# A gated-linear-attention block on one core: two column blocks of its input projection cut into groups of 512 columns, some of their steps by block sums

## The chip, the cores and the metric

The kernel runs on one core of one Trainium2 chip. The metric is the device time of one execution in microseconds, as the median of several runs. The span in a profile is the time from the first to the last instruction of the core; the execution that was profiled took a little longer than its span.

## The reference

One layer (DEPTH is 1) of a pre-RMSNorm residual trunk, on 256 tokens of width 2048, in float32:

```
def reference(x, ...):
    h = x
    h = h + _gla_mixer(_rmsnorm(h, gla_norm), gla_w_in, gla_w_gate_up, gla_b_gate, gla_o_norm, gla_w_out)
    h = h + _sq_relu_mlp(_rmsnorm(h, mlp_norm), mlp_w_up, mlp_w_down)
    return _rmsnorm(h, final_norm)

def _gla_mixer(h, ...):
    q, k, v, r, g_low = split(h @ w_in)                # 1024, 1024, 2048, 2048, 16 columns
    log_a = log_sigmoid(g_low @ w_gate_up + b_gate) / 16
    # chunks of 64 tokens, 4 heads of 256 (keys) and 512 (values)
    state = d_c * state + k_dec^T v ;  o = q state     # scan over 4 chunks
    o = o * rsqrt(mean(o * o) + EPS) * o_norm
    return (o * silu(r)) @ w_out                       # 2048 x 2048

def _sq_relu_mlp(h, w_up, w_down):
    a = relu(h @ w_up)                                 # 8192 columns
    return (a * a) @ w_down
```

## The kernel before

All 256 tokens are kept on the chip, as two tiles of 128 tokens (`t` = 0, 1). The 2048 rows of a weight are 16 tiles of 128 (`kt`), or 8 pairs of them (`kp`). Every float32 weight is loaded to a tile `raw`, split by ScalarE into a rounded part `hi` (L121) and by VectorE into the rest `lo = raw - hi` (L134, L168), and multiplied on TensorE in three terms: x.hi with w.hi, x.hi with w.lo, x.lo with w.hi. There are six `raw` tiles, and five `hi` and five `lo` slots; a step that wants a tile waits until an earlier step has let go of it. Weights are loaded through SyncE's queue, in order.

The stages, in order of time: the first value half and the gate's low-rank columns (`in_w_vg`, to about 50 us); two key halves and two query halves of 512 columns (`turned`, to about 140 us); the second value half with the scores (to about 190 us); the first gate half with attention (to about 252 us); the second gate half, in which the transposing of the attention output begins (to about 287 us); four output groups of 512 columns (`out_group`, to about 374 us); then the MLP, which the change doesn't touch.

The second value half and both gate halves are calls of `natural`: 1024 columns, one 128-row tile of weights a step, four PSUM banks (two token tiles x two halves of 512 columns). A product on TensorE has 128 rows, 128 tokens and 256 columns, so a step has 2 x 4 x 3 = 24 of them.

`out_group` takes a pair of row tiles and 512 columns a step. A plain step has 24 products as well. A step "by sums" multiplies the 2 x 2 blocks (row tiles by token tiles, row tiles by halves of 256 columns) with seven products in place of eight (Winograd's form of Strassen's method), each in three terms: 21 products. It needs sums of the activations (eight forms, of which four are the blocks themselves), and sums of the weights. One sum of the weights is made by a load that adds to `raw`, issued by GpSimd (L798, after the plain load has landed); the others are made by VectorE (`weight_sums`, L231 and L232), in place, after three quarters of the raw tile have been split for the products that need no sum. Then the sums are split in a second pair of slots (L121 with 512 columns, L829) and the remaining four block products, the "second part" of the step, follow after the products of the next step. Products of the sums collect in two banks of their own, which are combined on ScalarE and VectorE when the last of them is done (L835 to L840) and added to the two banks of the group (L843).

For six of the output groups' steps, the first and the sixth or so of groups 1 to 3, the weight sums are prepared earlier (`make_sums`, `MADE_OUT`, `MADE_AT`): a piece of `w_out` is loaded, summed and split in an earlier stage (L248 to L258), written to DRAM, and read back later (`pre`, L793), ready for TensorE.

Work beside the products is put between the steps: `pump` runs one entry of `side` and one of `jobs` after each step (of a row tile in `turned` and `natural`), in the order that these lists have. `issue_after` fixes the order of instructions on an engine; otherwise the order on each engine is made when the program is built. Attention (`attend`) has 6 products for the first token tile and 12 for the second of each of four heads, and then a chain ScalarE (square sum, L619), VectorE (L620), GpSimd (a power, L401), VectorE (L623) for its normalization. `xe` holds copies of two row tiles of x at another address; some steps after scores, transposes or a change of stage use them (`EVEN`, `row_x`).

The residual `h` is loaded at the start (L391), into 16 KB a partition that it keeps to the end; its square sum gives the first normalization (`token_ssq`, L404). It is first needed when the first output group's banks begin with it (`begin_out`, L726).

Of the kernel before, what the change touches and what calls it, by code (L numbers as in the profile page):

```python
# [32 lines left out]
P = 128  # L33
T = 256
NT = T // P
D = 2048
# [32 lines left out]
def tile_gla_mlp(ctx, tc, x, xt, cols, w_vg, w_in, w_gate, w_out, w_up, w_down, final_norm, out):  # L69
# [4 lines left out]
    mid = ctx.enter_context(tc.tile_pool(name="mid", bufs=1))  # L74
    wpool = ctx.enter_context(tc.tile_pool(name="wpool", bufs=5))
# [98 lines left out]
    def halves(o, x, w, first, last):  # L174

        n = w.shape[-1]
        for c in range(0, n, T) if n % T == 0 else (0,):
            m = slice(c, c + T) if n % T == 0 else slice(0, n)
            nc.tensor.matmul(o[:, m], x, w[:, m], start=first and c == 0, stop=last, skip_group_check=True)  # L179
# [82 lines left out]
    def make_all():  # L262
        pair = lambda w, c0, g: w[c0 : c0 + 2 * P, g * GT : (g + 1) * GT].rearrange("(i p) c -> p i c", p=P)
        todo = [make_sums((None, g, kp), pair(w_out, 2 * kp * P, g)) for g, kp in MADE_OUT]
        todo += [make_sums((ROUNDS - 1, g, kp), pair(w_down, (ROUNDS - 1) * MR + 2 * kp * P, g)) for g, kp in MADE_DOWN]
        jobs.extend([lambda: None] * 3 * (KT - 1))
        for at, (high, low) in zip(MADE_AT, todo):
            jobs[at], jobs[at + 1] = high, low
# [78 lines left out]
    x_loads = {0: 1, 1: 3, 3: 6, 6: 9, 9: 12, 12: KT}  # L347

    def input_tile(kt):
# [14 lines left out]
        return (pieces, pieces) if kt == 0 else ([(0, 512), (512, WMAX)], pieces) if kt == 1 else None  # L364
# [11 lines left out]
    h = const.tile([P, NT, D], F32, name="h")  # L376
# [11 lines left out]
    def load_h(t, half):  # L388
        c = slice(half * G, (half + 1) * G)
        with tc.issue_after(last_load[0].ins):  # L390
            nc.sync.dma_start(out=h[:, t, c], in_=x[t * P : (t + 1) * P, c])  # L391
# [6 lines left out]
    ms1 = st.tile([P, NT], F32, name="ms1")  # L398
# [4 lines left out]
    def token_ssq(t):  # L403
        nc.scalar.activation(  # L404
            kab[:, 0].rearrange("p b c -> p (b c)"), h[:, t, :], AF.Square,
            accum_out=ms1[:, t : t + 1],
        )
# [12 lines left out]
    side.extend([clear_gate] + [nothing] * 8 + [load_gate, lambda: load_h(0, 0), lambda: load_h(0, 1)])  # L420
    side.extend([lambda: (load_h(1, 0), load_h(1, 1), split_gate())])
# [126 lines left out]

    for half in range(2):
        acc = turned(stream_x, w_in, half * GT, even=())  # L550
# [9 lines left out]
    def scores(hd, banks=None):  # L560
# [3 lines left out]
        def mm(o, k, q):  # L564
            for c in range(2):
                nc.tensor.matmul(o, kab[:, k[0], c0 + c, k[1] : k[1] + P], q(qt[:, c0 + c]), start=c == 0, stop=c == 1)  # L566
# [21 lines left out]

    def two_scores(hd):
        spare = [psum_bank(i, "aux") for i in list(acc_free)[:2]]  # L590
# [3 lines left out]
    side.extend([nothing] * 4 + [lambda: two_scores(0), nothing, lambda: two_scores(2)])  # L594
# [30 lines left out]
    side.extend([lambda: None] + [lambda hd=hd, t=t: attend(hd, t) for hd in range(HEADS) for t in range(NT)])  # L625
# [14 lines left out]
    S3, S2, S1, S4, A12, A11, A22, A21 = range(8)  # L640

    def form_sums(f, tt):
        tt(f[:, S3], f[:, A21], f[:, A11], ALU.subtract)
        tt(f[:, S2 : S1 + 1], f[:, A22 : A22 + 1].to_broadcast([P, 2, P]), f[:, 0::7], ALU.add)
        tt(f[:, S4], f[:, A12], f[:, S2], ALU.subtract)

    FORMED = (0, 1, 6, 7)
    in_forms = lambda a: a.rearrange("p (f s) -> p f s", f=8)
# [35 lines left out]
    acc = natural(once_x, rows(w_in, 4 * KEYW), G, HALF, order=even_at(0, 6))  # L684
    flush()
    gate_out(acc, 0)
# [32 lines left out]
    two = lambda a: a.rearrange("p (f s) -> p f s", f=2)  # L719
# [15 lines left out]
    side.extend([nothing] * 7 + [lambda: begin_out(0)])  # L735
# [10 lines left out]
    @contextmanager  # L746
    def then_mm():
        with ExitStack() as order:
            if last_mm[0]:
                order.enter_context(tc.issue_after(last_mm[0]))  # L750
            yield
        last_mm[0] = newest[0]

    made_o = []

    def out_group(g, order, summed, between):

        tt = nc.vector.tensor_tensor
        banks = [out_banks[g, t] for t in range(NT)]
        sums_banks = []  # L760
        begun = set()
        pending = None
        block = lambda i, n=1: slice(i * T, (i + n) * T)

        def product(bank, o, a, w, n, last=False):
            for x in a[: 2 - n]:
                for d in range(0, w.shape[-1], T):
                    newest[0] = nc.tensor.matmul(  # L768
                        bank[:, o + d : o + d + T], x, w[:, d : d + T],
                        start=bank in sums_banks and bank.name not in begun, stop=last, skip_group_check=True,  # L770
                    ).ins
                    begun.add(bank.name)

        def products(these, w, last=False):
            with then_mm():
                for n in range(2):
                    for bank, o, a, c in these:
                        product(bank, o, a, w[n][:, c], n, last and n == 1)

        for step, kp in enumerate(order):  # L780
            by = kp in summed
            ready = made.get((None, g, kp))
            raw = raw_tile()[:, : 2 * GT]
            src = w_out[2 * kp * P : 2 * (kp + 1) * P, g * GT : (g + 1) * GT].rearrange("(i p) c -> p i c", p=P)
            if ready is not None:
                if not made_o:
                    made_o.extend(big.tile([P, 4 * G + 64], F32R, tag="C", name="pre")[:, : 4 * G].rearrange("p (b i c) -> b p i c", b=2, i=2))
                ready_in = made_o[0]
                made_o.reverse()
                last_load[0] = nc.sync.dma_start(out=raw[:, T:GT], in_=src[:, 0, T:])  # L790
                last_load[0] = nc.sync.dma_start(out=raw[:, GT:], in_=src[:, 1])
                for i in range(2):
                    last_load[0] = nc.sync.dma_start(out=ready_in[:, i].bitcast(F32), in_=ready[i])  # L793
                ready = [ready_in[:, i] for i in range(2)]
            elif by:
                for i in range(2):
                    last_load[0] = nc.sync.dma_start(out=raw[:, i * GT : (i + 1) * GT], in_=src[:, i])
                nc.gpsimd.dma_start(out=raw[:, :T], in_=src[:, 0, T:], accum_op=ALU.add)  # L798
            else:
                last_load[0] = nc.sync.dma_start(out=raw.rearrange("p (i c) -> p i c", i=2), in_=src)  # L800
            w = parts(raw, 2 * GT, slots(), [(T * by, 2 * GT)])
            if by:
# [572 lines left out]
```

## Time and profile before

| | |
|---|---|
| median of 3 runs | 1042.85 us (1042.48 to 1043.14) |
| the profiled execution | 1043.0 us |
| its span | 1041.1 us |
| granted TensorE clock | 0.999 |
| instructions in the span | 23253 |
| DMA traffic | 241.48 MB, mean 232 GB/s |

The page of the profile gives, for each engine, its busy time and share of the span. PE is TensorE's matmuls, PEld its weight loads, DVE is VectorE, ACT ScalarE, POOL GpSimd, SP SyncE; a "q" behind the name is the queue that issues DMAs. A row of a group of instructions reads: line, engine, operation, written tile <- read tiles, shapes, count | busy us, mean ns of one | idle us of the engine just before them, and what ended that idle time. A row of a timeline begins with start and length in us. A row of a stage view reads: stage, its length, then busy time (and count of instructions) of PE, PEld, DVE, ACT and POOL, the granted clock, the share of the 16 DMA engines and GB/s. A row of DMA issues ends with KB of each and the median us to landing.

### The profile page before, as it was taken

To read this page: it belongs to the slowest core of one execution; us is meant where nothing else is said; L and a number is where in the kernel's file an instruction comes from. 1 tells how busy PE (TensorE), PEld (TensorE's weight loads), DVE (VectorE), ACT (ScalarE), POOL (GpSimd) and SP (SyncE) were. 2 spreads that over 40 slices of the span, in tenths; PEclk is the share of its full clock that TensorE was granted. 3 is DMA by queue.
4 is the path that set the end of the run, shared out by engine and by line. 5 is a ranking of instruction groups with operands and counts; after the bars stand their busy time and mean duration, and the time that the engine had idled before them with its cause. 6 is when DMAs were issued, how large, how long until landed. Compare 5 with 4: busy or idle time off the path is not lost.

```text
span 1041.1 us, 23253 instructions
## 1 busy us (share of the span) xinstructions
PE 1032.0 (99%) x9046; PEld 1031.4 (99%) x9046; DVE 874.6 (84%) x1191; ACT 738.5 (71%) x1091; POOL 126.9 (12%) x173
## 2 busy tenths in 40 slices
PE   9999999999999999999999999999999999999997
PEld 9999999999999999999999999999999999999997
DVE  6668665667698876989999999999999999999887
ACT  7675554546586755677779788778788778778685
POOL 0000000120100001111111111111111111111000
PEclk9999999999999999999999999999999999999999
DMA  9966676665979976678887888887888888887772
GB/s 339 331 193 190 196 253 213 219 222 167 317 233 296 301 250 197 180 211 232 225 247 226 230 234 224 240 236 224 248 225 228 239 229 228 240 232 220 231 245 84
DMA packets 123742, 241.48 MB, mean 232 GB/s; under 512 B 11200, under 2 KB 28480, under 8 KB 123504
## 3 DMA queue, kind: packets, MB, share of 16 engines
q1 hardware_dynamic: 103616, 216.11, 64.7%
q0 software_dynamic: 19296, 22.29, 11.6%
q10 hardware_dynamic: 720, 1.60, 0.4%
q8 instruction: 71, 1.16, 0.4%
q14 instruction: 39, 0.32, 0.1%
HBM read 231.56 MB, written 8.39 MB: 230 GB/s over the span
## 4 chain that ended last, share of the span: by engine, by line
PE 98%; DMA 1%; issue 0%; ACT 0%; SPq 0%; DVE 0%; POOLq 0%; POOL 0%; DVEq 0%
PE up L923 33%; PE acc L923 28%; PE acc L179 18%; PE acc L768 8%; PE acc L222 6%; PE aux L222 2%; PE aux L179 1%; PE aux L667 1%; PE aux L566 1%; DMA raw<-in_w_vg 1%; ACT sqf L1262 0%; SPq L171 0%; PE acc L467 0%; SPq L356 0%; DVE hf L1334 0%
## 5 line engine op out<-in xcount | busy, mean ns | idle before, releaser
L121 ACT CAST hi<-raw 128x768 fp32r<-128x768 f32 (+4 forms) x630 | 507.0, 834 | 207.1 <-DVE raw L231 61.5
L134 DVE TENSOR_TENSOR lo<-raw,hi 128x768 fp32r<-128x768 f32 (+3 forms) x226 | 236.0, 1051 | 82.9 <-ACT hi L121 71.8
L923 PE MATMUL acc<-hi,act 128*128 128x256 f32 x1696 | 247.7, 276 | 0.0
L923 PE MATMUL up<-hh,hi 128*128 128x256 f32 x1024 | 238.7, 276 | 0.0
L923 PE MATMUL up<-hl,hi 128*128 128x256 f32 x1024 | 238.7, 276 | 0.0
L168 DVE TENSOR_TENSOR lo<-raw,hi 128x1024 fp32r<-128x1024 f32 x160 | 194.7, 1219 | 29.1 <-ACT hi L121 28.6
L923 PEld LDWEIGHTS acc<-hi,act 128*128 128x128 f32 x1696 | 217.6, 188 | 0.0
L923 PEld LDWEIGHTS up<-hl,hi 128*128 128x128 f32 x1024 | 192.2, 188 | 0.0
L923 PEld LDWEIGHTS up<-hh,hi 128*128 128x128 f32 x1024 | 192.2, 188 | 0.0
L1133 POOL DMA_DIRECT2D raw<-in_w_down x112 | 97.1, 867 | 518.0 <-DMA raw<-in_w_down 225.3
L1193 DVE TENSOR_TENSOR lo<-raw,hi 128x1024 fp32r<-128x1024 f32 x112 | 136.4, 1218 | 1.1 <-ACT hi L121 1.1
L923 PE MATMUL up<-hh,lo 128*128 128x256 f32 x1024 | 137.0, 276 | 0.0
L923 PE MATMUL acc<-lo,act 128*128 128x256 f32 x848 | 133.8, 276 | 0.0
L923 PEld LDWEIGHTS up<-hh,lo 128*128 128x128 f32 x1024 | 125.7, 188 | 0.0
L923 PEld LDWEIGHTS acc<-lo,act 128*128 128x128 f32 x848 | 113.4, 188 | 0.0
L179 PE MATMUL acc<-hi,xA 128*128 128x256 f32 (+1 forms) x736 | 105.5, 278 | 0.6 <-ACT hi L121 0.6
L179 PEld LDWEIGHTS acc<-hi,xA 128*128 128x128 f32 x736 | 94.2, 188 | 1.0 <-ACT hi L121 1.0
L232 DVE TENSOR_TENSOR raw<-raw 128x512 f32<-128x512 f32 x128 | 88.3, 690 | 3.4
L231 DVE TENSOR_TENSOR raw<-raw 128x256 f32<-128x256 f32 x128 | 54.1, 423 | 11.5 <-DMA raw<-in_w_out 8.5
L179 PE MATMUL acc<-lo,xA 128*128 128x256 f32 (+1 forms) x368 | 61.8, 278 | 0.0
L179 PEld LDWEIGHTS acc<-lo,xA 128*128 128x128 f32 x368 | 51.0, 188 | 0.0
L222 PE MATMUL acc<-xA,hi 128*128 128x256 f32 x288 | 49.2, 276 | 0.0
(194 smaller groups left out, 1241.4 us busy)
## 6 DMA issues: line engine op xcount, KB each, us to landing
raw<-in_w_up SPq DMA_DIRECT2D x128, 512.0 KB, 4.5
raw<-in_w_down SPq DMA_DIRECT2D x224, 256.0 KB, 4.4
raw<-in_w_in SPq DMA_DIRECT2D x80, 512.0 KB, 4.5
raw<-in_w_down POOLq DMA_DIRECT2D x112, 128.0 KB, 5.1
raw<-in_w_out SPq DMA_DIRECT2D x22, 512.0 KB, 5.1
raw<-in_w_down SPq DMA_DIRECT2D x16, 512.0 KB, 5.0
raw<-in_w_vg SPq DMA_DIRECT2D x14, 520.0 KB, 8.6
raw<-in_w_out SPq DMA_DIRECT2D x26, 256.0 KB, 5.4
```

The source lines that it names most:

```text
L121: last_hi[0] = nc.scalar.copy(to, raw)
L134: last_lo[0] = nc.vector.tensor_tensor(lo[:, s], raw[:, s], hi[:, s].bitcast(F32), op=ALU.subtract)
L168: last_lo[0] = nc.vector.tensor_tensor(to[1], dst, to[0].bitcast(F32), op=ALU.subtract)
L179: nc.tensor.matmul(o[:, m], x, w[:, m], start=first and c == 0, stop=last, skip_group_check=True)
L222: nc.tensor.matmul(o, u[:, i, s], m, start=kt == 0 and n == 0 and j % 2 == 0, stop=kt == KT - 1 and n == 2, skip_group_check=True,)
L231: nc.vector.tensor_tensor(u[:, 2], u[:, 0], u[:, 2], op=ALU.subtract)
L232: return nc.vector.tensor_tensor(u[:, 1::2], u[:, 1::2], u[:, 2:3].to_broadcast([P, 2, T]), op=ALU.subtract)
L566: nc.tensor.matmul(o, kab[:, k[0], c0 + c, k[1] : k[1] + P], q(qt[:, c0 + c]), start=c == 0, stop=c == 1)
L768: newest[0] = nc.tensor.matmul(bank[:, o + d : o + d + T], x, w[:, d : d + T], start=bank in sums_banks and bank.name not in begun, stop=l ...
L923: newest[0] = nc.tensor.matmul(o, x, w, start=first, stop=last, skip_group_check=True).ins
L1133: nc.gpsimd.dma_start(out=raw[:, :T], in_=src[:, 0, T:], accum_op=ALU.add)
L1193: last_lo[0] = nc.vector.tensor_tensor(to[1][:, :G], u, to[0][:, :G].bitcast(F32), op=ALU.subtract)
```

## The change

The second value half and the first gate half (2 x 1024 columns) become four groups of 512 columns, V0, V1, G0 and G1, each of eight steps over a pair of row tiles, by the same function that serves the output groups (now `group`). For three pairs of x (0, 1 and 4) the eight forms are made from the transposed x during the first stage (`make_x`); the four sums among them are kept in the place of the residual, the blocks are x itself. Two steps of V0 and three of V1, G0 and G1 are by sums; each of these steps loads its first 128 x 256 piece a second time, adding, through GpSimd. The scores stand between the steps of V0, six of the eight attention blocks between those of G0, the last two in G1. The results of the sums are combined in a buffer where the last quarter of the residual will lie.

The residual is loaded in the second gate half, after its steps 6 to 9, in four pieces into the four places that the three x forms and the combining buffer had. The square sum at the start reads a copy of x loaded at the old time into the keys' buffer.

Five steps of the output groups are prepared in place of six (the first step of output group 1 is not), three of them in the second query half and two in the second gate half as before. At the start one tile of x in place of two is loaded ahead of the second weights, and the third weights are split in three pieces.

```
-    MADE_OUT = ((1, 1), (1, 6), (2, 1), (2, 6), (3, 1), (3, 6))
-    MADE_AT = (1, 5, 19, 24, 36, 40)
+    MADE_OUT = ((1, 6), (2, 1), (2, 6), (3, 1), (3, 6))
+    MADE_AT = ((0, 5, 10), (6, 10))
...
-    x_loads = {0: 1, 1: 3, 3: 6, 6: 9, 9: 12, 12: KT}
+    x_loads = {0: 1, 1: 2, 2: 4, 4: 7, 7: 10, 10: 13, 13: KT}
...
-        return (pieces, pieces) if kt == 0 else ([(0, 512), (512, WMAX)], pieces) if kt == 1 else None
+        loads = {0: pieces, 1: [(0, 512), (512, WMAX)], 2: [(0, WMAX)]}
+        return (loads[kt], pieces) if kt in loads else None
...
-    h = const.tile([P, NT, D], F32, name="h")
+    x_forms = {kp: shared.tile([P, G], F32R, tag=f"h{i}", name="xf")... for i, kp in enumerate(X_FORMED)}
...
+    def load_x(t, half):
+        c = slice(half * G, (half + 1) * G)
+        with tc.issue_after(last_load[0].ins):
+            nc.sync.dma_start(out=k_rows[:, t, c], in_=x[t * P : (t + 1) * P, c])
+
+    def load_h(t, half):
+        h[t, half] = shared.tile([P, G], F32, tag=f"h{2 * half + t}", name="h")
+        with tc.issue_after(last_load[0].ins):
+            nc.sync.dma_start(out=h.get((t, half)), in_=x[t * P : (t + 1) * P, half * G : (half + 1) * G])
...
+    def make_x(kp):
+        f = in_forms(wpool.tile([P, G], F32, tag="more", name="form", bufs=1))
+        for i in range(2):
+            kt = 2 * kp + i
+            nc.scalar.activation(f[:, A12 + 1 - i :: 2], xr[:, kt, :]..., AF.Copy, scale=g1(kt))
+        form_sums(f, lambda o, x, y, op: nc.vector.tensor_tensor(o, x, y, op=op))
+        sh, sl = (x_forms[kp][:, i] for i in range(2))
+        nc.scalar.copy(sh, f[:, :A12])
+        nc.vector.tensor_tensor(sl, f[:, :A12], sh.bitcast(F32), op=ALU.subtract)
...
-    make_all()
-    acc = natural(row_x, rows(w_in, 3 * KEYW), G, HALF, order=even_at(9, 11))
-    flush()
-    for t in range(NT):
-        for c in range(2):
-            put_v(acc[t][c], 512, t, G + 512 * c)
+    def x_group(n, c0, order, summed, between, put, rows_of={}):
+        def combine(p16, p57):
+            nc.scalar.copy(comb_x[:, 1::2], two(p16))
+            nc.scalar.copy(comb_x[:, 0::2], two(p57))
+            # four sums of 256 columns on VectorE
+        def put_all(banks):
+            for t in range(NT):
+                o = comb_x[:, 2 * t : 2 * t + 2]
+                nc.vector.tensor_tensor(o, two(banks[t]), o, op=ALU.add)
+                put(o.rearrange("p f s -> p (f s)"), t)
...
+    V0 = (5, 0, 6, 2, 4, 3, 7, 1), (0, 4)
+    V1 = (2, 5, 0, 3, 4, 6, 1, 7), (0, 4, 1)
+    G0 = (2, 5, 0, 3, 4, 6, 1, 7), (0, 4, 1)
+    G1 = (2, 0, 5, 4, 3, 1, 6, 7), (0, 4, 1)
+    x_group(0, 3 * KEYW, *V0, {
+        **{i: lambda i=i: [f() for f in rest[2 * i : 2 * i + 2]] for i in range(2)},
+        2: lambda: two_scores(0), 4: lambda: two_scores(2),
+    }, at_of_v(0), FIRST)
+    x_group(1, 3 * KEYW + GT, *V1, {}, at_of_v(GT))
...
+    x_group(2, 4 * KEYW, *G0, {i + 1: f for i, f in enumerate(attends[:6])}, gate_x(0), {2: FIRST[2]})
+    x_group(3, 4 * KEYW + GT, *G1, {i: f for i, f in enumerate(attends[6:])}, gate_x(GT))
...
-    acc = natural(once_x, rows(w_in, 4 * KEYW), G, HALF, order=even_at(0, 6))
-    flush()
-    gate_out(acc, 0)
...
-    side.extend([nothing] * 7 + [lambda: begin_out(0)])
+    side.extend([nothing] * 3 + [lambda i=i: load_h(i % 2, i // 2) for i in range(4)] + [lambda: begin_out(0)])
```

The body of `group` is that of `out_group` before, with what differs between the output and the x groups passed in (the banks, the forms, how the sums are combined and where the result goes).

More of the change, by code (lines that the diff above doesn't have):

```diff
@@ L35 @@
 NT = T // P
+X_FORMED = (0, 1, 4)
 D = 2048
@@ L547, in extend_q @@
         )
+    make = make_all()
     for half in range(2):
+        if half:
+            jobs.extend(next(make))
         acc = turned(stream_x, w_in, half * GT, even=())
```

284 lines of the change are left out of this document (169 added, 115 removed).

## The prediction

> **What bounds the kernel now.** I read the page first (busy shares, then the chain that ended last), then TensorE's own waits, then stages. From the page:
>
> ```profile
> PE 1032.0 (99%) x9046; PEld 1031.4 (99%) x9046; DVE 874.6 (84%) x1191; ACT 738.5 (71%) x1091; POOL 126.9 (12%) x173
> ...
> PE 98%; DMA 1%; issue 0%; ACT 0%; SPq 0%; DVE 0%; POOLq 0%; POOL 0%; DVEq 0%
> ```
>
> TensorE's waits in the whole execution:
>
> ```profile
> core 0 of [0], span 1041.1 us
> engine line waited for: us in total, times, longest us
> PE aux L295 <- DVE ones L292: 1.1, 1, 1.1
> PE acc L179 <- ACT hi L121: 0.6, 2, 0.4
> ```
>
> TensorE is busy 99% of the span, 98% of the chain is its own, and after the warm-up it waits twice, 0.6 us together. So a matmul taken out of the stream shortens the kernel by its full spacing, provided that no new wait appears. A piece of the chain in which nothing interrupts gives the spacing:
>
> ```profile
> 75.20 65.36 PE acc L222 x576
> ```
>
> 65.36 / 576 = 0.1135 us for a 128x128x256 product. The change can save only products, and it can lose only by making TensorE wait or by making its products slower.
>
> **The change part by part.** *Products.* A plain step over a pair of 128-row tiles takes 2 row tiles x 2 token tiles x 2 column quarters x 3 terms = 24 products; a step by sums takes 7 block products x 3 terms = 21. The lists in the code hold 2 + 3 + 3 + 3 = 11 steps by sums (the change's few words say ten). 11 x 3 = 33 products go; 33 x 0.1135 = 3.75 us. Attention, scores and transposes keep their number. With ten steps it would be 3.40 us.
>
> *What VectorE and ScalarE do for a step by sums.* The output groups (287 to 374 us) work this way already, so their rows price it:
>
> ```profile
> L134 DVE TENSOR_TENSOR lo<-raw,hi 128x1024 fp32r<-128x1024 f32 x14 | 16.8, 1219 | 1.2 <-ACT hi L121 0.6 <-DMA pre<-made 0.5
> L134 DVE TENSOR_TENSOR lo<-raw,hi 128x768 fp32r<-128x768 f32 x15 | 14.2, 951 | 0.1
> L829 DVE TENSOR_TENSOR lo<-raw,hi 128x1024 fp32r<-128x1024 f32 x10 | 12.2, 1217 | 1.2 <-ACT hi L121 1.1
> L232 DVE TENSOR_TENSOR raw<-raw 128x512 f32<-128x512 f32 x9 | 6.2, 688 | 0.2
> ...
> L843 DVE TENSOR_TENSOR h<-acc,some 128x512 f32<-128x512 f32 x8 | 5.2, 682 | 0.0
> ...
> L231 DVE TENSOR_TENSOR raw<-raw 128x256 f32<-128x256 f32 x9 | 3.8, 422 | 7.2 <-DMA raw<-in_w_out 7.1
> ```
>
> On VectorE a plain step costs 1.22 us, a step by sums 0.95 + 0.42 + 0.69 + 1.22 = 3.28 us. A group with three of them costs 3 x 3.28 + 5 x 1.22 = 15.9 us, then four combining sums of 256 columns, as L231's (4 x 0.42 = 1.7), two additions to the banks (2 x 0.68 = 1.4) and two evacuations. For these and for attention, from 140 to 260 us:
>
> ```profile
> L623 DVE TENSOR_SCALAR on<-aux,r1k,ors 128x512 f32<-128x512 f32 x8 | 6.5, 808 | 3.5 <-POOL ors L401 3.5
> ...
> L431 DVE SCALAR_TENSOR_TENSOR vl<-acc,r,vh 128x512 fp32r<-128x512 f32 x4 | 2.7, 745 | 0.0
> ```
>
> Two evacuations of values cost 1.5 us (the gate's, two of the 0.68 kind, 1.4), so a group comes to 20.5 us of VectorE against (3 x 21 + 5 x 24) x 0.1135 = 20.8 us of TensorE. In G0 six attention blocks add 6 x 0.81 = 4.9 us to VectorE and 54 products, 6.1 us, to TensorE. On paper VectorE therefore fits with 1 to 7% to spare. In the first value group, with two steps by sums and all the scores, there is more room. Whether such a fit holds in practice is shown by the stretch 287 to 309, the first output group, in the next view:
>
> ```profile
> core 0: us, PE busy (x) PEld busy (x) DVE busy (x) ACT busy (x) POOL busy (x), PEclk, DMA share, GB/s
> 108.00:140.00 32.00, 32.00 (x285) 32.00 (x284) 20.46 (x37) 14.18 (x19) 3.08 (x17) 1.00 0.67 207
> 190.00:252.00 62.00, 62.00 (x549) 62.00 (x548) 41.89 (x57) 33.41 (x49) 9.23 (x12) 1.00 0.67 217
> 248.00:268.00 20.00, 20.00 (x179) 20.00 (x178) 15.95 (x25) 13.54 (x20) 1.64 (x3) 1.00 0.64 218
> 268.00:287.00 19.00, 19.00 (x170) 19.00 (x170) 12.01 (x12) 9.19 (x11) 3.79 (x5) 1.00 0.94 316
> 287.00:309.00 22.00, 22.00 (x196) 22.00 (x195) 21.51 (x34) 17.65 (x30) 1.11 (x2) 1.00 0.71 233
> ```
>
> There VectorE is busy 21.51 of 22.00 us and TensorE still 22.00: four steps by sums and two transposing turns were hidden. The new groups ask for less. I cost the x groups' VectorE and ScalarE work at nothing on the path; it is hidden by the products. If the cover is gone the price is the overhang: TensorE would stand 1 us per group for every 5% that VectorE loses to waits.
>
> *The group for which one prepared step is dropped.* Output group 1 must now form the sums of its first step: 0.42 + 0.69 + 1.22 = 2.33 us more on VectorE, right behind the stretch that is full. How much room is there? VectorE first, then TensorE's first use of the same `lo` tiles (the third row of VectorE opens with the tile for 324.58; the first of the second fence is the one for 305.93):
>
> ```profile
> 304.57 1.22 DVE L134 TENSOR_TENSOR lo<-raw,hi 128x1024 fp32r<-128x1024 f32 x1
> ...
> 319.94 1.21 DVE L829 TENSOR_TENSOR lo<-raw,hi 128x1024 fp32r<-128x1024 f32 x1
> 321.07 5.22 DVE L134 TENSOR_TENSOR lo<-raw,hi 128x1024 fp32r<-128x1024 f32 x5
> ```
>
> ```profile
> 305.93 0.41 PE L768 MATMUL acc<-lo,oth 128*128 128x256 f32 x2
> ...
> 324.58 0.39 PE L768 MATMUL acc<-lo,oth 128*128 128x256 f32 x2
> ```
>
> The tile used at 305.93 is ready at 305.79: 0.14 us of room, the tightest place of this part. The tile used at 324.58 begins at 321.07 and takes 1.22 us, ready at 322.29: 2.29 us of room. Of the 2.33 us added, back-to-back starts are some 7% shorter than durations (from 319.94 to 321.07 is 1.13 for 1.21), so about 2.15 us arrive, and the room shrinks to about 0.1. Bounds: 0 if it fits, 2.3 if the added work comes in a bunch with other late work. I take 0.2.
>
> *The residual loaded late.* Four loads of 128 x 1024 x 4 B, 2.1 MB, now stand in SyncE's queue in steps 6 to 9 of the second gate half, ahead of the output groups' first weights; the early loads at the start stay (into the keys' buffer). From 248 to 287 the rows carry 20 x 0.218 + 19 x 0.316 = 10.4 MB; with 2.1 more, 12.5 MB in 39 us or 320 GB/s, and most of it should come before 268, where the DMA share is 0.64. What the engines can carry is seen at the start:
>
> ```profile
> 0.00:20.00 20.00, 18.36 (x136) 17.93 (x137) 12.66 (x22) 14.21 (x25) 1.77 (x9) 1.00 0.91 337
> 20.00:40.00 20.00, 20.00 (x169) 20.00 (x168) 13.11 (x16) 13.51 (x20) 0.00 (x0) 1.00 1.03 391
> ```
>
> 391 GB/s, so on average it fits. If all of it fell into 268 to 287, 6.0 + 2.1 = 8.1 MB would need 20.7 us at 391 GB/s instead of 19: 1.7 us late, and the group behind it has 0.14 us of room. Bounds 0 and 1.7; I take 0.3. The last of the four also waits until the combining buffer in the same place is free; behind it in SyncE's queue stand weight loads for some 20 us ahead, which is its cover.
>
> *Prepared steps in the second query half.* Three of the five now run there, five 12-product passes apart (5 x 12 x 0.1135 = 6.8 us). Each costs VectorE 0.42 + 0.42 + 0.69 + 1.22 = 2.75 us; the plain steps in 6.8 us cost 2.5 x 1.22 = 3.1. From 108 to 140 VectorE is idle 11.5 of 32 us, so 8.3 us fit. Their traffic, 3 x (0.5 read + 1.05 written) = 4.7 MB, lifts 6.6 MB in that stretch to 11.3, or 354 GB/s. The rate of 391 above holds it. The Trainium skill (DMA: Bandwidth & Descriptors, Specifications) gives about 358 GB/s as a core's share of HBM; by that figure this stretch would just fit too, but 268 to 287 would be late by 3.6 us instead of 1.7. The measured 391 GB/s is over the figure, and I go by it. On the path I take 0 for this part, with 0 and 1 as bounds.
>
> *The start.* One tile of x instead of two is loaded ahead of the second weights:
>
> ```profile
> 6.31 0.91 ACT L370 ACTIVATE xA<-zz,colt 128x256 fp32r<-128x256 f32 x2 [0.80 <-DMA zz<-in_xt]
> 7.38 0.71 ACT L121 CAST hi<-raw 128x256 fp32r<-128x256 f32 x2 [0.16 <-DMA raw<-in_w_vg]
> ```
>
> Both rows wait for DMA, and behind them TensorE has its 0.6 us of waits. 131 KB less at 337 GB/s come 0.39 us earlier. Gain between 0 and 0.6; I take 0.4. Making the sums of x (three times some 2 us on VectorE by the rows for 256 and 512 columns, between 20 and 40 us where it is busy 13.11 of 20) is off the path. The prefetch after that runs ahead of TensorE, so nothing is lost again.
>
> **The sum**, against the profiled execution's 1043.0 us (span 1041.1): -3.75 - 0.4 + 0.2 + 0.3 and 0.2 for small waits at the four group borders = -3.45, so 1039.6. The median of the runs shown is 0.15 lower than the profiled time: 1039.4.
>
> **The rivals.** *A: VectorE becomes the bound in the new groups.* For it: 20.5 against 20.8 us leaves nothing for waits, and from 190 to 252 VectorE idles 20 of 62 us although there is room ahead of it. Against: 287 to 309. If 5% are lost in V1, G0 and G1, 3 us come back: 1042.4, within 0.2% of before.
>
> *B: the handover to the output groups.* The loads fall late (1.7 us) and group 1 has no room (2.3 us): 1039.4 - 0.5 + 4.0 = 1042.9, also no change that can be told. By the page's 358 GB/s it would be 1.9 us more, 1044.8.
>
> *C: the accumulating loads stand behind attention on GpSimd's queue.* In G0 three steps by sums need a load that adds to `raw`, issued by GpSimd, and six attention blocks need a power on the same in-order queue. Rows:
>
> ```profile
> L401 POOL TENSOR_TENSOR ors<-oss,mhalf 128x1 f32<-128x1 f32 x8 | 7.0, 876 | 13.3 <-DVE oss L620 13.1
> ```
>
> ```profile
> L798 POOL DMA_DIRECT2D raw<-in_w_out x7 | 6.0, 864 | 60.8 <-DVE lo L134 23.5 <-DVE raw L232 16.8 <-DMA raw<-in_w_out 16.2
> ```
>
> ```profile
> raw<-in_w_out POOLq DMA_DIRECT2D x10, 128.0 KB, 5.8
> ```
>
> The power already waits 13.1 us for VectorE's `oss`, which needs TensorE's attention product. A load queued behind it starts only then: 0.88 + 0.86 + 5.8 + 0.42 + 0.69 + 1.22 and ScalarE's two copies (about 1.2, an estimate from VectorE's 0.68 for as many columns) = 11.1 us until the second part of the step can run, while TensorE has 9 + 9 + 24 products, 4.8 us, to do. Each such step stalls 6.3 us. One stall ends at 1045.7, slower by over 0.2%; three at 1058. It decides from the first step whose load the order puts behind a power; the order is made when the program is built and the trace of before cannot show it. Against: L798's row shows loads going out when their tile has landed (16.2 us of its waits), long before TensorE needs them.
>
> *D: the change doesn't pay because products get slower.* With 272-column products among them, 20 to 40 us holds 169 products where 248 to 268 holds 179. If the new groups' 735 products ran at the first stage's spacing (20/169, less 1.25% for the wider ones, 0.117 us), 735 x 0.0033 = 2.4 us come back: 1041.8, no change that can be told from the runs, or little more than that.
>
> **How the numbers follow.** About 0.2% (2.1 us) is what a measurement of this kernel can tell from no change, so faster means under 1040.8. Forecast, at most 1.2 us of further waits: 0.62. A 0.07, B 0.07, D 0.04: these are 0.18 of no change. C, or several of A and B together, is 0.20 of slower. Predicted 1039.4. Low end 1038.0: all 3.75 and 0.6 gained, no stall (1038.5), and the spread of the runs. The high end takes in A, B and D and stops at one stall of C, 1045.7.
>
> **What would show it.** Right: TensorE's products fall from 9046 by about 33, its waits stay below 2 us, the spacing stays 0.1135, the first output group starts some 4 us earlier, VectorE is busy about 90% in the four groups. Wrong: waits of PE on `lo` of L134 or of the second parts in G0 (C), on `lo` in the first two output groups (B), waits evenly in V1 to G1 (A), or fewer than 176 products in 20 us (D). A wait over 2 us in any one place breaks the forecast.

## The result and the profile after

The changed kernel takes 1044.54 us (median of 20 runs, 1042.42 to 1048.72), the kernel before 1043.38 us beside it (1042.48 to 1045.41): a ratio of 1.0017, 95% interval 1.0009 to 1.0024. Nothing was gained, and a little lost. (Below, differences between versions are taken from such ratios, of 1043 us.) The runs of the changed kernel also lie further apart, 6.3 us against 2.9.

The execution that was profiled took 1045.65 us (span 1043.9), 1.1 us over the median of its kernel, so the figures below are those of one of its slower executions. From its page, busy shares and the chain that ended last:

```profile
PE 1032.6 (99%) x9013; PEld 1031.0 (99%) x9013; DVE 908.7 (87%) x1261; ACT 755.5 (72%) x1133; POOL 135.0 (13%) x183
...
PE 94%; DVE 2%; DMA 1%; issue 1%; ACT 1%; POOL 0%; POOLq 0%; DVEq 0%; ACTq 0%
```

The 33 products are gone (9046 to 9013). But the chain, 98% TensorE's own before, now leaves TensorE for 6% of the span. TensorE's waits:

```profile
PE aux L697 <- PE aux L697: 0.8, 1, 0.8
PE acc L305 <- DVE lo L365: 0.5, 1, 0.5
PE acc L305 <- DVE lo L136: 0.5, 1, 0.5
PE aux L697 <- DVE at L712: 0.4, 1, 0.4
PE acc L305 <- ACT hi L123: 0.2, 1, 0.2
```

L305 is the product of `group`, L697 that of the scores; none of these waits stood in the profile before. They are 2.4 us together, the loss is larger. The first products of each stage in the trace show where it lies (us of the profiled executions; the last three columns are versions from the experiments below). The second border is the first product behind the transposes at about 250 us; these stand behind the first three steps of the second gate half, which begins at 241.8 us in the changed kernel, so the second row holds these steps as well:

| | before | changed | e3 | e9 | e14 |
|---|---|---|---|---|---|
| start to G0's first product | 190.22 | 192.10 | 188.73 | 187.98 | 187.88 |
| G0, G1, three steps of the second gate half | 61.59 | 59.50 | 59.50 | 59.51 | 59.51 |
| rest of the second gate half | 35.52 | 35.52 | 35.51 | 35.52 | 35.51 |
| output group 0 | 28.37 | 28.75 | 28.74 | 28.75 | 28.69 |
| output group 1 | 21.35 | 23.83 | 21.35 | 21.35 | 21.35 |
| from there to the end of the span | 704.07 | 704.19 | 704.27 | 704.26 | 704.27 |

G0 and G1 pay what was forecast: 18 products less, 2.09 us. Up to G0's start 15 products and 0.4 us of the start should have brought 2.1 us; 1.9 were lost. Output group 1 lost 2.5 more.

Part of the loss is not in waits. Three stretches: the first two are of the changed kernel, the end of V0 with most of V1 (which begins at about 170.5 us), then the end of G1 with the beginning of the second gate half; the third is nearly all V1, of e9:

```profile
165.00:188.00 23.00, 23.00 (x198) 23.00 (x197) 19.55 (x26) 13.94 (x20) 2.10 (x3) 1.00 0.61 164
225.00:248.00 23.00, 23.00 (x205) 23.00 (x204) 20.94 (x28) 16.17 (x21) 1.70 (x2) 1.00 0.77 246
```

```profile
165.00:188.00 23.00, 23.00 (x206) 23.00 (x205) 19.24 (x25) 13.26 (x18) 1.72 (x2) 1.00 0.66 184
```

TensorE is busy 23.00 of 23.00 us in each, at a granted clock of 1.00, and does 198 products in one and 205 or 206 in the others. In the trace the starts of products lie 113 or 114 ns apart in the latter (113.3 mean) and 117 to 119 ns in the former (117.8, called 118 below). From 143.7 to 192.8, 305.7 to 318.5 and 322.9 to 342.0 us the changed kernel runs at 118 ns. In the kernel before only the first stage does so for long, and later only the few products around scores, transposes and changes of stage. A busy share can't show this; the count in a stretch does.

### The profile page after: what moved, and what is told of

It reads as the page before. It is cut to its first block, busy times and chain, and to the rows that moved or that the text cites. A ratio compares the mean times of both kernels' runs of the same rounds, so it can differ in the third digit from the quotient of the medians.

```text
span 1043.9 us, 23395 instructions
## 1 busy us (share of the span) xinstructions
PE 1032.6 (99%) x9013; PEld 1031.0 (99%) x9013; DVE 908.7 (87%) x1261; ACT 755.5 (72%) x1133; POOL 135.0 (13%) x183
## 4 chain that ended last, share of the span: by engine, by line
PE 94%; DVE 2%; DMA 1%; issue 1%; ACT 1%; POOL 0%; POOLq 0%; DVEq 0%; ACTq 0%
PE up L1022 33%; PE acc L1022 28%; PE acc L305 14%; PE acc L181 10%; PE acc L224 5%; PE aux L224 2%; DVE lo L136 1%; DMA made<-hi 1%; PE aux L181 1%; PE aux L844 1%; DMA raw<-in_w_in 0%; ACT hi L123 0%; PE aux L399 0%; PE aux L697 0%; DVE lo L170 0%
## 5 line engine op out<-in xcount | busy, mean ns | idle before, releaser
L123 ACT CAST hi<-raw 128x512 fp32r<-128x512 f32 (+4 forms) x656 | 518.6, 821 | 201.6 <-DVE raw L233 70.8
L136 DVE TENSOR_TENSOR lo<-raw,hi 128x768 fp32r<-128x768 f32 (+4 forms) x228 | 232.7, 1031 | 53.7 <-ACT hi L123 49.4
L1022 PEld LDWEIGHTS acc<-lo,act 128*128 128x128 f32 x848 | 113.3, 188 | 0.0
L234 DVE TENSOR_TENSOR raw<-raw 128x512 f32<-128x512 f32 x139 | 96.0, 690 | 3.5
L233 DVE TENSOR_TENSOR raw<-raw 128x256 f32<-128x256 f32 x139 | 58.8, 423 | 7.7 <-DMA raw<-in_w_out 4.7
L181 PE MATMUL acc<-hi,xA 128*128 128x256 f32 (+1 forms) x376 | 56.0, 281 | 0.0
L181 PEld LDWEIGHTS acc<-hi,xA 128*128 128x128 f32 x376 | 49.9, 190 | 0.0
L224 PEld LDWEIGHTS acc<-xA,hi 128*128 128x128 f32 x288 | 43.4, 188 | 0.0
L1149 ACT COPY sums<-acc 128x512 f32<-128x512 f32 x46 | 26.9, 584 | 22.4 <-PE acc L1022 22.4
```

What stands on the lines that cost most here:

```text
L123: last_hi[0] = nc.scalar.copy(to, raw)
L136: last_lo[0] = nc.vector.tensor_tensor(lo[:, s], raw[:, s], hi[:, s].bitcast(F32), op=ALU.subtract)
L181: newest[0] = nc.tensor.matmul(o[:, m], x, w[:, m], start=first and c == 0, stop=last, skip_group_check=True).ins
L224: nc.tensor.matmul(o, u[:, i, s], m, start=kt == 0 and n == 0 and j % 2 == 0, stop=kt == KT - 1 and n == 2, skip_group_check=True,)
L233: nc.vector.tensor_tensor(u[:, 2], u[:, 0], u[:, 2], op=ALU.subtract)
L234: return nc.vector.tensor_tensor(u[:, 1::2], u[:, 1::2], u[:, 2:3].to_broadcast([P, 2, T]), op=ALU.subtract)
```

## The experiments

**What held TensorE up in V0.** Timeline of GpSimd's queue, then of ScalarE, changed kernel:

```profile
133.52 0.90 POOL L335 DMA_DIRECT2D raw<-in_w_in  x1 [3.01 <-DMA raw<-in_w_in]
134.09 0.88 POOL L256 DMA_DIRECT2D made<-hi  x1
```

```profile
130.32 1.05 ACT L255 CAST hi<-raw 128x1024 fp32r<-128x1024 f32 x1 [5.13 <-DVE raw L234]
131.27 2.94 ACT L123 CAST hi<-raw 128x1024 fp32r<-128x1024 f32 x3
134.69 0.84 ACT L123 CAST hi<-raw 128x768 fp32r<-128x768 f32 x1 [0.47 <-PE acc L224]
142.57 1.05 ACT L123 CAST hi<-raw 128x1024 fp32r<-128x1024 f32 x1 [7.05 <-DMA made<-hi]
```

The last prepared step of the query half has its `hi` tile at 131.37. Its store is issued by GpSimd only at 134.09, behind V0's first accumulating load (L335), which waits 3.01 us for a plain load to land. The store lands at 142.50, 8.4 us later. Meanwhile four more splits have used up the other four `hi` slots, and the next must have the slot that is being stored: ScalarE stands 7.05 us.

**e1: the store ahead of the load.**

```
-    MADE_AT = ((0, 5, 10), (6, 10))
+    MADE_AT = ((0, 4, 8), (6, 10))
```

> Only the places of the three prepared steps in the second query half change: 0, 4 and 8 instead of 0, 5 and 10, so that the last one's store of its hi tile is issued by GpSimd ahead of the first accumulating load of V0 and not behind it. Theory (hi slot): in the changed kernel that store is issued at 134.09 us, 2.7 us after its tile was made, lands 8.4 us later and holds a hi slot, so ScalarE stands 7.05 us before 142.57 and TensorE loses 4.0 us in V0 and V1 (2.6 us of waits, 1.4 us of products at 118 instead of 113 ns). With the store early, ScalarE's idle time before V0's third split falls below 3 us, the waits of TensorE from 143 to 160 us fall below 0.5 us, and the time falls by about 4 us, to some 2.8 us under the kernel before. Rival (VectorE's load): three prepared steps in one half are too much work wherever they stand, or the steps by sums themselves are late; then the waits stay and the time stays within 1 us of the changed kernel's, 1.2 us over the kernel before.

Measured: 1043.19 us against 1043.09 beside it, ratio 1.0001 (0.9992 to 1.0009). The queue and the split that had waited:

```profile
129.63 0.53 POOL L256 DMA_DIRECT2D made<-hi  x1
132.15 0.90 POOL L335 DMA_DIRECT2D raw<-in_w_in  x1 [1.99 <-DMA raw<-in_w_in]
```

```profile
133.45 0.84 ACT L123 CAST hi<-raw 128x768 fp32r<-128x768 f32 x1 [0.53 <-DMA made<-hi]
136.62 1.05 ACT L123 CAST hi<-raw 128x1024 fp32r<-128x1024 f32 x1 [2.34 <-DMA raw<-in_w_in]
```

ScalarE's wait for the store falls from 7.05 to 0.53 us, TensorE has no wait left from 143 to 160 us, and the runs lie 1.5 us apart in place of 6.3. So the late store held V0 up, and not three prepared steps as such; the edit moves the last step's work on VectorE forward as well, but ScalarE's wait of 7.05 us names the store. But only 1.7 us came back (1.0001 against 1.0017), not 4: TensorE still ran at 118 ns from 147.6, where the scores are, to G0's start, and new waits came in output groups 0 and 1. My theory had put the spacing down to the wait; that was wrong.

**e2: six prepared steps** (the first of group 1 back).

```
-    MADE_OUT = ((1, 6), (2, 1), ...
+    MADE_OUT = ((1, 1), (1, 6), (2, 1), ...
-    MADE_AT = ((0, 5, 10), (6, 10))
+    MADE_AT = ((0, 5, 10), (2, 6, 10))
```

> The sixth prepared step, the first of output group 1, is put back (three prepared steps in the second gate half, at 2, 6 and 10); the rest is the changed kernel. Theory (no room in group 1): the 2.33 us of VectorE work and two splits on ScalarE that this step needs are what makes TensorE wait 1.9 us between 316 and 327 us and run at 118 ns for some 20 us; with the step prepared, output group 1 takes 21.4 us again instead of 23.8 and the time is 2.5 us under the changed kernel's, about 1.3 us under the kernel before. Rival (late residual loads make the handover late): group 1 stays above 23 us and the time within 0.5 us of the changed kernel's.

Measured: 1044.2 us (1039.82 to 1044.84), ratio 1.0007 (0.9999 to 1.0016): 1.0 us less than the changed kernel where 2.5 were expected, and the two intervals overlap. Its profiled execution, 1041.64 us, has group 1 at 22.10 us, and what is over 21.35 there is one wait at the transposes that begin it, for group 0's results. The medians alone don't settle it: this version still has the late store, and its runs spread over 5 us.

**e5: the other way round**, the kernel before with five prepared steps:

```
-    MADE_OUT = ((1, 1), (1, 6), (2, 1), ...
+    MADE_OUT = ((1, 6), (2, 1), ...
-    MADE_AT = (1, 5, 19, 24, 36, 40)
+    MADE_AT = (5, 19, 24, 36, 40)
```

> The kernel before, with only the first step of output group 1 no longer prepared (five prepared steps; the other five at their old places). Theory (no room in group 1): the same waits as in the changed kernel, on the sums and their lo and hi tiles around 316 to 327 us, and a stretch at 118 ns behind them: 2.5 us over the kernel before. By the prediction's sum (2.15 us of work into 2.29 us of room) it would be 0.2 us over it.

Measured: 1045.84 us (1045.58 to 1046.29), ratio 1.0027 (1.0016 to 1.0038), or 2.8 us (2.75 by the medians). Group 1 takes 23.82 us, with the waits of the changed kernel:

```profile
323.69 1.24 PE L768 MATMUL acc<-hi,of 128*128 128x256 f32 x8 [0.24 <-ACT hi L121]
325.46 0.74 PE L768 MATMUL acc<-lo,of 128*128 128x256 f32 x4 [0.53 <-DVE lo L829]
```

So this edit alone costs more than the whole change lost. VectorE in the changed kernel at that place:

```profile
318.72 1.23 DVE L365 TENSOR_TENSOR lo<-raw,hi 128x1024 fp32r<-128x1024 f32 x1
320.49 0.96 DVE L136 TENSOR_TENSOR lo<-raw,hi 128x768 fp32r<-128x768 f32 x1 [0.55 <-ACT hi L123]
321.48 0.42 DVE L233 TENSOR_TENSOR raw<-raw 128x256 f32<-128x256 f32 x1
321.84 0.96 DVE L136 TENSOR_TENSOR lo<-raw,hi 128x768 fp32r<-128x768 f32 x1
322.72 0.69 DVE L234 TENSOR_TENSOR raw<-raw 128x512 f32<-128x512 f32 x1
323.32 0.87 DVE L858 SCALAR_TENSOR_TENSOR hl<-aux,colt,hh 128x256 fp32r<-128x256 f32 x2
324.22 1.22 DVE L365 TENSOR_TENSOR lo<-raw,hi 128x1024 fp32r<-128x1024 f32 x1
```

The tile that TensorE waits for at 325.5 is begun at 324.22. Ahead of it stand a wait for ScalarE and the second half of the transposed residual (L858): the work for this step goes back and forth between the two engines.

**e3: both edits.**

> Both edits: the last store of the second query half early (places 0, 4 and 8) and six prepared steps. If the two losses are separate and are all that was lost, 4.0 + 2.5 us come back: 6.5 us under the changed kernel, 5.3 us under the kernel before, or about 1038.1 us. If the prepared work in the second gate half (three steps with four loads of the residual beside them) makes a new wait there, or the x groups are bound by VectorE, less than 4 us come back in all.

Measured: 1040.92 us, ratio 0.9982 (0.9973 to 0.999): 1.9 us under the kernel before (2.2 by the medians), 3.7 under the changed one; 6.5 had been expected. The profile has no wait of TensorE behind the warm-up, and group 1 is at 21.35 us. But V0 and V1 run at 118 ns from 147 to 189 us, without any wait, and from 302 to 312 us group 0 does. (This execution is the fastest of its eleven, which reach to 1043.99.)

**What sets the spacing.** The kernel has copies of some x tiles at another address (`xe`); it takes them after scores or at a change of stage. In the kernel before, twelve products with such a copy follow the scores, and the thirteenth starts at 113 ns. V0 has a step of half the width, so only six.

e4, on the changed kernel: V1 begins with such a copy.

```
-    x_group(1, ..., *V1, {}, at_of_v(GT))
+    x_group(1, ..., *V1, {}, at_of_v(GT), {2: FIRST[2]})
```

> Only TensorE's first six products of V1 change: they take the copy of the x tile at the other address and the other token tile first, as V0 after the scores and G0 at its start do. No wait is touched. Theory (a spacing that stays): after a wait TensorE's 256-column products start 118 ns apart instead of 113 and stay so until such a place; V1's about 180 products come back to 113 ns after the first six, 180 x 4.5 ns = 0.8 us less than the changed kernel. Rival (the spacing belongs to the operands of the x groups or to the load on the memories): V1 stays at 118 ns and the time within 0.3 us.

Measured: 1044.05 us, ratio 1.0012 (1.0003 to 1.002), 0.5 us under the changed kernel, which the runs can't tell from nothing. The profiled execution was already at 113 ns from 159.6 us on, behind the second scores and only six products, so its trace can't tell either. The same edit on e3 can:

> The version with the early store and six prepared steps, and V1 beginning with the copy of x at the other address. In the profile of the version without this last edit V0's rest and all of V1 ran at 118 ns although nothing waited there: 210 products of V1 at 118 in place of 113.5 ns. Theory: V1 comes back to 113.5 ns, 0.9 us less, 3.1 us under the kernel before (about 1040.0 us). Rival (another place inherits the spacing): nothing changes from that version's 2.2 us under the kernel before.

Measured: 1040.17 us, ratio 0.9971 (0.9959 to 0.9982), 1.1 us under e3. The profile is at 118 ns from 147.8 until 168.6 us, six products of V1 behind its beginning, and at 113 from there. From the key stage to G0 it takes 129.09 us where e3 takes 129.88, with no wait touched. The two intervals of the runs overlap, so the 1.1 us are no closer than that; and this edit swaps the order of two row tiles together with the address, so it doesn't show the address alone.

e9, on e3 without that edit: one more tile (7) is copied, so that twelve products with copies follow the second scores.

```
+    xe7 = xe_gt[:, 3 * T :].rearrange("p (i s) -> p i s", i=2)
...
+        # in split_input: tile 7's first 128 tokens are copied to xe7, as 5 and 6 to xe
...
-            return (row_x if (kt, t) in ...
+            return [xe7[:, i] for i in range(2)] if 3 in rows_of and (kt, t) == (7, 0) else (row_x if (kt, t) in ...
```

> The version with the early store and six prepared steps (V1 without the extra place); after the second pair of scores the first twelve products, not six, take copies of x at the other address (one more tile is copied for this in the first stage). In the kernel before, twelve such products follow the scores and the spacing is 113 ns right after them; in the changed kernel there are six, and it stays 118 ns in the profiles without a wait there. Theory (six are too few behind the scores): V0's rest and V1 run at 113.5 ns: about 270 products x 4.5 ns = 1.2 us less than the version without it, 3.4 us under the kernel before. Rival (the number doesn't matter, only the phase in which the scores leave TensorE): no change from 2.2 us under it, and 118 ns from 157 to 189 us.

Measured: 1039.63 us, ratio 0.9972 (0.9961 to 0.9982), 1.0 us under e3 (expected 1.2), again with overlapping intervals; from the key stage to G0 the profile takes 128.75 us, 1.1 less than e3's. Here only addresses change. The spacing is 113 ns from 159.1, right behind the twelve. The stretch of e9 that was shown above has 206 products; the same one of e3 has 197, at the same busy share of the DMA engines:

```profile
165.00:188.00 23.00, 23.00 (x197) 23.00 (x197) 18.77 (x23) 12.47 (x17) 1.72 (x2) 1.00 0.66 175
```

Behind the second scores and six products the spacing stayed at 118 in the changed kernel, e1, e2, e3 and e6 and came back in e4; behind twelve it came back in all eight profiles that have them.

e12: twelve behind the first scores, too (tile 4).

> The version with twelve products behind the second pair of scores, with twelve behind the first pair too (one more tile copied at the other address, during the first query half). Theory (twelve bring the spacing back, six do not): the 47 products and the scores between 150 and 157 us: only some 30 products more at 113.5 ns, and V0 begins its second scores 0.1 to 0.4 us earlier; 0.1 to 0.4 us less than the version without it, about 1039.4 us. Rival: 118 ns stays there as in that version; no difference.

Measured: 1039.9 us, ratio 0.9968 (0.9956 to 0.9981), no difference from e9 that the runs can tell. The profile is at 113 ns from 152.0 to 154.3, as expected. G0 began 0.15 us earlier than in e9, and group 0 took 29.66 us with a wait of TensorE for VectorE near 300:

```profile
PE acc L305 <- DVE lo L365: 0.4, 1, 0.4
```

e11, on the kernel before: tiles 5 and 6 of the first stage are taken from their copies.

```
-    acc = natural(plain_x, rows(w_vg, 0, WMAX), ...
+    acc = natural(row_x, rows(w_vg, 0, WMAX), ...
```

> The kernel before, with two tiles of the first stage (5 and 6, first token tile) taken from their copies at the other address. That stage runs at 118 ns from its start to 60 us (349 products of 256 columns). Theory (the spacing stays until such a place, wherever it began): behind tile 6, at about 25 us, some 220 products come back to 113.5 ns: 1.0 us less than before, 1042.1 us. Rival (the 272-column products in every step of this stage put it back to 118 ns each time, or make it): no difference, 118 ns up to 60 us.

Measured: 1043.24 us, ratio 1.0001 (0.9992 to 1.001). The products come to 113 ns at 23.8 us and are back at 118 at 25.6. The rival was right: the steps of this stage, each with 272-column products, don't keep the 113 ns.

**The start.** e8, the kernel before with the changed `x_loads` and `loads` alone.

> The kernel before with only the start of the changed one: one tile of x ahead of the second weights, the third weights split in three. Prediction's term: 0.4 us less (0 to 0.6). In the three profiles so far the key stage begins 0.4 to 1.0 us earlier than before, the more, the fewer of the first products ran at half rate; so 0.4 to 0.9 us less, about 1042.6 us. Rival: the start belongs to how the clock comes up in each execution and not to the loads; then no difference.

Measured: 1043.34 us, ratio 1.0005 (0.9996 to 1.0014): nothing gained that the runs can tell, as the rival had it. In the profile it was 0.88 us ahead of the kernel before up to group 0's first product (286.45 against 287.33); then group 0 ran at 118 ns (28.74 us), and group 1 began with a new wait for group 0's results:

```profile
PE aux L668 <- DVE h L844: 0.6, 1, 0.6
```

**The steps by sums.** e13: e9 with one such step in V1, G0 and G1 each.

```
-    V1 = (...), (0, 4, 1)        # G0, G1 likewise
+    V1 = (...), (0,)
```

> The version with twelve products behind the second scores, but with one step by sums in V1, G0 and G1 each in place of three: 18 products more, five steps by sums in place of eleven, all else as in that version. If VectorE's and ScalarE's work for the sums lies wholly beside TensorE there, the time is 18 x 0.1135 = 2.04 us longer than that version, 1041.7 us. If that work costs something on the path (rival A, VectorE the bound), less than 2.04 us is lost, at the full price of A (3 us) nothing or a gain of 1 us.

Measured: 1041.07 us, ratio 0.9982 (0.9974 to 0.9991), 1.0 us over e9 by the ratios and 1.4 by the medians, less than the 2.04. In the profiles the stages give the full price: the second row of the table takes 60.87 in place of 59.51 us (1.36 for 12 products), and from the first key product to G0's it is 0.69 more for six: 2.05 in all. So by the profiles the sums cost nothing on the path in these stages, which speaks against rival A. The runs alone don't settle it: their intervals leave room for 2.04 us and for less than 1. The two profiled executions as a whole are 2.9 us apart, more than the runs, with 0.5 of it in group 1, where nothing was changed.

**Group 0.** e14: e12 with three steps by sums in group 0 in place of four.

```
-    out_group(0, ORDER[0], FORMED, {
+    out_group(0, ORDER[0], (0, 6, 7), {
```

> The version with twelve products behind both pairs of scores; in output group 0 pair 1 is taken plainly, so three steps by sums there in place of four: 3 products more (0.34 us) and 2.06 us of VectorE's work less between 283 and 302 us. Theory (VectorE has no room in output group 0, whatever comes early is given back there): no wait of TensorE on a lo tile near 300 us and none at the transposes of group 1, spacing 113.5 ns through group 0 (97 products x 4.5 ns = 0.44 us); 0.1 to 0.8 us less than the version without it, 1039.1 to 1039.8 us. Rival (the wait near 300 us has another cause, the loads or the order): the wait and the 118 ns stay and the time is 0.34 us longer, about 1040.2 us.

Measured: 1039.25 us (1039.02 to 1041.08), ratio 0.9967 (0.9956 to 0.9978), 3.4 us under the kernel before, the lowest of all though not to be told from e9 and e12. The wait near 300 us and the one at the transposes are gone. In the stretch from 303 to 312 us, first in the changed kernel, then here:

```profile
303.00:312.00 9.00, 9.00 (x80) 9.00 (x79) 8.28 (x12) 6.36 (x11) 1.71 (x2) 1.00 0.74 224
```

```profile
303.00:312.00 9.00, 9.00 (x82) 9.00 (x81) 8.04 (x13) 6.27 (x11) 0.85 (x1) 1.00 0.87 261
```

80 products become 82: 113 ns all through group 0, which takes 28.69 us with three products more. In e12 VectorE works without a pause of 0.1 us from 294 to 303 us, and TensorE waits for its `lo` tile in that stretch; so VectorE's work is what group 0 has no room for there. The edit takes two splits from ScalarE as well, and it is one profile. The kernel before has 82 products in the same stretch, with four steps by sums:

```profile
303.00:312.00 9.00, 9.00 (x82) 9.00 (x81) 8.86 (x11) 6.96 (x11) 1.50 (x2) 1.00 0.67 190
```

Of the thirteen profiles with four steps by sums in group 0, it is the only one in which 113 ns last through the group. So the 0.4 us that group 0 takes longer in the changed kernel may belong to the execution of the kernel before that was profiled, and not to the change.

## Why the prediction was right and wrong

The forecast, 1039.4 us and faster, was wrong; the measured 1044.54 lies in the range, near its upper end, and at a ratio (1.0017) that I had called no change. That it lies in the range is luck: the upper end stood for a stall of rival C in G0, and no trace shows one.

**Right.** 33 products went, and where nothing else happened each was worth its spacing: 2.09 us in G0 and G1, 2.05 for the 18 of e13. The x groups' VectorE and ScalarE work lies beside TensorE (VectorE 20.94 of 23.00 us from 225 to 248, most of it G1, no wait). The late residual, put at 0.3 us with 1.7 as its bound, cost nothing: the rest of the second gate half takes 35.52 us with it and without, and the longer group 0 (28.75) stands as well in e5, e8 and e11, where the residual is loaded at the start. What the loads alone would cost was not tried. The borders between the groups, put at 0.2, show no wait.

**Wrong: "On the path I take 0" for the prepared steps in the second query half.** They cost the waits in V0: from the key stage to G0 the profiled execution takes 132.65 us where e3 takes 129.88, 2.8 us and over my bound of 1. (In e2, whose store landed sooner, it is 130.56, so the price differs between executions; that fits the wide spread of the runs.) I had set mean work against mean idle time, on VectorE and on the DMA engines. What ran out was neither, but a `hi` slot: a tile that is stored keeps its slot until the store has landed, and the store stood in GpSimd's queue behind an accumulating load. Rival C had this queue and this kind of load, but in G0 and with a power ahead of it. I had looked at that queue for the loads alone: the stores of the moved steps are on it, too.

**Wrong: "Of the 2.33 us added ... the room shrinks to about 0.1. ... I take 0.2".** Alone it costs 2.75 us in the runs (e5) and 2.47 in the profile's group 1, over the upper bound of 2.3. I had measured the room at one tile (324.58) and counted VectorE alone. The step also needs two 512-column splits on ScalarE, the chain of splits and sums goes through both engines from group 0 on, and the last stall is followed by some 14 us at 118 ns (0.5 us in group 1). Rival B had this place and about this price (2.3 us); its other half, late loads, didn't come.

**Wrong: the spacing.** I had used 0.1135 us everywhere and gave rival D 0.04. D was right in kind and wrong in cause: not the new products, but scores without enough products at the other address behind them put V0 and V1 at 118 ns, 1.1 us between the profiles of e3 and e9. With that repaired in e9 the runs are 1.0 us shorter, which agrees but isn't clear of noise. A row that warned of it was there: I had taken the 169 products in 20 us of the first stage for the effect of 272 columns alone, and not counted the copies behind the scores.

**The start**, 0.4 us, is there in the profile (the key stage begins at 59.45 in place of 59.84) and on the average of all profiles: 59.31 in the eleven with the new start (58.85 to 59.99) against 59.70 in the three with the old one. Alone it gave nothing in the runs. What comes early before group 0 can be given back there. Of the 4.15 us that products and start should bring, the repaired versions with six prepared steps show 2.9 (e9) to 3.4 (e14). In the profiles group 0 keeps 0.4 us of it, or three products are given for it; the rest isn't accounted for.

Of my own later theories, that a wait sets the 118 ns in V0 fell with e1. Open is why six products are mostly too few behind the scores and enough at V1's and G0's beginnings, why group 0 took 28.37 us in the profile before and 28.74 to 28.75 in e5 and e11, which issue the same work there or nearly so, and why the same store took 3.8 us to land in e1 and, by the start of the split that waited for it, 6.4, 6.8 and 8.5 us in e2, e4 and the changed kernel, where it is issued late.

## What to carry to other kernels

When work is moved, list every slot it holds and until which event, and every queue that its stores and loads join; a mean share of 64% on an engine (VectorE's from 108 to 140 us before) says nothing of the one tile that waits for a store. Measure room along the whole chain of engines that make a tile, not at one tile on one of them, and follow saved time to the next place without room, where it may be given back. Where an engine is busy 99%, count its instructions per stretch: a 4% longer spacing is invisible in the busy share and cost some 2.3 us in the changed kernel's profile (an estimate from 4.5 ns each for about 520 products in V0, V1 and groups 0 and 1).

## What the runs showed of the hardware

TensorE's 256-column products have two spacings at the same granted clock of 1.00, 113.3 and 118 ns on average, and keep the one they are in for tens of microseconds. The 118 ns are seen behind scores, behind stalls (one of 17 ns near 305.7 us in the changed kernel, though the kernel before had the same one and stayed at 113) and in steps with 272 columns (e11). Products with a stationary tile at another address lead back: six at the beginnings of V1 and G0, twelve behind the scores (six sufficed there in e4 alone). What makes the difference in TensorE isn't shown. The Trainium skill (TensorE: Matmul & The Clock Gate, Back-to-back issue gap) gives one spacing for lone products, 262 cycles at 2.4 GHz for 256 columns, an estimate of 109 ns, and says that in a stream the loads of the stationary tile count as well; here both spacings are longer.

The first products of the first stage run at 213 ns, and how many of them do differs between executions with the same start: at most one in e3, six in the changed kernel, eleven in e13. They end where the trace has its first record of the full clock (at 5.9 us in the changed kernel, 7.1 in e13). The key stage begins at 58.85 us in e3, 59.45 in the changed kernel and 59.99 in e13. The same page (What's actually happening) says that the number of slow products at the start varies from run to run; the traces agree.
